# Early weight parts at listed places, stored from ScalarE's queue; layer 1's modulation pieces further apart; two squares summed on TensorE

## The chip, the cores and the metric

One NeuronCore of a Trainium2 chip runs the kernel. The metric is the device time of one execution in microseconds (us); the time of a kernel is the median of its runs. The profile is of one further execution, with a time of its own. A core's engines work side by side: TensorE (PE; its weight loads are listed as PEld) for matrix products, VectorE (DVE), ScalarE (ACT) and GpSimd (POOL) for elementwise work, SyncE (SP), whose queue issues most transfers.

## The reference

Two layers over two streams of 256 tokens by 1024 features in float32: the latent stream `x` and a context stream `ctx`. Each layer is a modulated RMSNorm, a mixer with a gated residual, and a modulated RMSNorm with a gated ConvFFN. Layer 0's mixer is a bidirectional retention with four heads, layer 1's a bidirectional recurrent block (RG-LRU).

```python
silu_c, silu_cc = jax.nn.silu(c), jax.nn.silu(c_ctx)
for i in range(DEPTH):
    need_ctx = i < DEPTH - 1
    mod_l = (silu_c @ ada_w[i] + ada_b[i])[:, None, :]
    mod_c = silu_cc @ ada_w[i] + ada_b[i]
    sh1, sc1, g1, sh2, sc2, g2 = jnp.split(mod_l, N_MOD, axis=-1)
    ...
    h_l = modulate(rmsnorm(x, norm_mix[i]), sh1, sc1)
    h_c = modulate(rmsnorm(ctx, norm_mix[i]), csh1, csc1)
    out_c, out_l = ...
    x = x + g1 * out_l
    ...
    x = x + g2 * conv_ffn(modulate(rmsnorm(x, norm_ffn[i]), sh2, sc2), ...)
    ...
return rmsnorm(x, final_norm)
```

## The kernel before

The features lie on the 128 partitions and the tokens of both streams side by side, 512 columns in all (`NT`), 256 of each stream (`NS`). Each weight matrix is cut into blocks of 128 by 128. A float32 product is made of three faster ones: the weight is split into a high part (`whi`) and a low part (`wlo`), the activation likewise, and `mm3` (L515 to L518) multiplies high by high, high by low and low by high into one sum (`ps`).

The weights are streamed in the order in which they are used, in units of eight blocks (1024 columns, 512 KB). SyncE's queue loads a unit into one of nine `raw` buffers (L394); ScalarE casts it to `whi` (L417), VectorE subtracts to get `wlo` (L449), and TensorE multiplies it into the activations. A raw buffer can be loaded again when its last reader is done, and the loads stand in one order on SyncE's queue. `make_plan` (L88) writes this order down: the list `PIECES`, with marks every 16 blocks. Beside the blocks it puts two other kinds of pieces there.

- **Modulation pieces** ("ada"). The rows of `ada_w` are multiplied by the two condition vectors: ScalarE scales 512 columns (L570, L573), GpSimd adds the result to a sum (L574). Up to four such products are taken from the queue `adaq` at each tick; a tick comes once per matrix product of eight blocks (`tick`, L356). At the end the sums go through TensorE with a ones vector (`total`, L588), are copied by ScalarE (`down`, L601) and transposed by four small products (`up`, L607) into `mod`. `need` waits, in the program's order, until a group is done. `L1` sets where the two groups of layer 1 (l1 for the mixer, f1 for the FFN) are read: l1 from block 576 on, every 16 blocks, f1 from 768 on.
- **Early weight parts** ("pre"). The recurrent block's own 40 units (130 to 169) are loaded and split long before they are used, when there is time, written back to memory and later loaded as ready parts (`kept`, L482). ScalarE casts the high part (L467), VectorE subtracts the low part (L474) and copies back some blocks of 32 rows (L477), and SyncE stores both at once (L482). `pre_piece` (L453) queues these as three steps of `preq`, one per tick, and the store two ticks later (`keepq`). `PRE = (64, 48)` reads a piece (two units) at blocks 64, 112, 160 and so on to 976.

A gemm of layer 0's FFN is followed on VectorE by the two side taps of a convolution (`cv`, L1182 and L1183), a product of gate and value (L1191) and the low part of that (`fzlo`, L539).

At the end of the retention and of layer 0's FFN the next RMSNorm's sum of squares is built: ScalarE squares each of eight chunks (`sq`, L653), GpSimd adds them up (L659) but for the last one, and TensorE sums over the partitions with a matrix of ones (`st`, L663 for the sum, L665 for the last square). ScalarE takes the root (`sd`, L671), VectorE the reciprocal (`rstd`, L673). `direct` is the number of squares that TensorE takes without GpSimd. `staged_out` (L1027) does the last part of such a matrix for one stream after the other (s = 0, then 1), `staged_in` the first part of the next.

Of the kernel before, what the change touches and what calls it, by code (L numbers as in the profile page):

```python
# [12 lines left out]
P = 128  # L13
# [47 lines left out]
L1 = (64,16,256,16)  # L61
# [34 lines left out]
def make_plan():  # L96
# [78 lines left out]
    for n, i in enumerate(range(first, last, 16)):  # L175
        early.setdefault((PRE[0] + PRE[1] * n) // 16 * 16, []).append(i)
# [84 lines left out]
PRE = (64, 48)  # L261
# [34 lines left out]
class Net:  # L296
# [59 lines left out]
    def tick(self, n=1):  # L356
# [8 lines left out]
        if self.keepq and self.keepq[0][0] <= self.now:  # L365
            self.keepq.popleft()[1]()
# [11 lines left out]
    def load(self, upto):  # L378

        while self.nload <= min(upto, len(LOADS) - 1):  # L380
# [10 lines left out]
            while any(t <= n - RAWS for t, _ in self.preq):  # L391
                self.preq.popleft()[1]()
            r = self.wp.tile([P, UNIT], F32, tag="raw", name=f"raw{pi}{'ab'[h]}", bufs=RAWS)
# [59 lines left out]
    def pre_piece(self, pi):  # L453

        nc = self.nc
        rs = [self.half(pi, h) for h in range(2)]
        st = {}

        def hi(h, u):
            while len(self.keepq) > 1:  # L460
                self.keepq.popleft()[1]()
            st[h] = t = self.wp.tile([P, 2, UNIT], F32R, tag="pre", name=f"pre{u}", bufs=2)
            r, o = rs[h], 0
            cuts = [(a, n) for kind, a, n in self.runs(u) if kind == "main"] + [(UNIT, UNIT)]
            for a, n in cuts:
                if a > o:
                    nc.scalar.copy(t[:, 0, o:a], r[:, o:a])  # L467
                if n > a:
                    nc.scalar.copy(t[:, 0, a:n].bitcast(F32), r[:, a:n])
                o = n  # L470

        def lo(h, u):
            t = st[h]
            nc.vector.tensor_tensor(t[:, 1, :], rs[h], t[:, 0, :].bitcast(F32), ALU.subtract)  # L474
            for kind, a, n in self.runs(u):
                if kind == "left":
                    nc.vector.tensor_copy(t[64:96, 0, a:n], t[64:96, 1, a:n])  # L477
            self.keepq.append((self.now + 2, lambda: keep(h, u)))

        def keep(h, u):  # L480
            self.kept[u] = self.dp.tile([P, 2, UNIT], F32, tag=f"kept{u}", name=f"kept{u}")
            nc.sync.dma_start(self.kept[u], st[h].bitcast(F32))  # L482

        u = PIECES[pi][1] // 8
        a, b = (PLACE[pi, h][1] for h in range(2))
# [160 lines left out]
    def stats_begin(self, direct=1):  # L646
# [380 lines left out]
    def staged_out(self, name, ks, ms, rhs, layer, p, nxt):  # L1027
# [6 lines left out]
        for s in range(2):  # L1034
            sl = slice(s * NS, (s + 1) * NS)
            for i, m in enumerate(ms):
# [12 lines left out]
                self.residual(ps[:, :NS], layer, p, m, s)  # L1049
                self.stats_add(m, s)  # L1050
# [732 lines left out]
```

## Time and profile before

| | |
|---|---|
| time, median of 3 runs | 1240.64 us (1240.56 to 1242.41) |
| the profiled execution: time, span | 1242.04 us, 1240.2 us |
| TensorE: busy, mean granted clock | 1190.2 us (96%), 0.984 |
| VectorE, ScalarE, GpSimd: busy | 899.3 us (73%), 730.9 us (59%), 365.5 us (29%) |
| chain that ended last: TensorE, VectorE, DMA | 74%, 15%, 4% |

An engine's busy time is the sum over its instructions, and a share of it is an average over stages with different limits. The chain that ended last is followed back from the last instruction: each piece of it is what the next one waited for. Where TensorE's own instructions are the chain, nothing held it. The time of a run is some 2 us above the span, for what lies before the first and after the last instruction.

### The profile page before, as it was taken

What the parts mean: (1) busy time and instruction counts of PE and PEld (TensorE: products, weight loads), DVE (VectorE), ACT (ScalarE), POOL (GpSimd) and SP (SyncE); (2) the same over time, 40 slices, a digit from 0 to 9 for tenths busy, and PEclk for the clock granted to TensorE, in tenths of its full rate; (3) what the DMA queues carried; (4) which work ended last, traced back from release to release, by engine and by line L of the source; (5) the groups of instructions that cost most, each with busy time, mean ns of one, the idle gap of its engine ahead of it and who ended that gap; (6) DMA issues with size and microseconds to landing.
All of it is one profiled execution on the core that took longest, in us unless ns stands there. A gap on an engine that the chain in (4) does not pass through costs nothing.

```text
span 1240.2 us, 17983 instructions
## 1 busy us (share of the span) xinstructions
PE 1190.2 (96%) x6760; PEld 1012.2 (82%) x6760; DVE 899.3 (73%) x1285; ACT 730.9 (59%) x1098; POOL 365.5 (29%) x242
## 2 busy tenths in 40 slices
PE   8999799999979998988999999999999999999997
PEld 4678688778868888876778887879989888999996
DVE  5665977895596578899953678743758877988843
ACT  5456466765654444878754676432397856766542
POOL 0000545558160022489954355221000001000010
PEclk9999899999999999999989999999999999999999
DMA  9963577377355254577688688744576895555531
GB/s 327 337 236 133 172 265 242 119 270 256 101 171 204 97 210 141 200 270 256 220 314 286 232 286 291 252 136 136 185 288 220 310 324 186 172 187 185 190 117 34
DMA packets 73399, 265.37 MB, mean 214 GB/s; under 512 B 8672, under 2 KB 12384, under 8 KB 68192
## 3 DMA queue, kind: packets, MB, share of 16 engines
q1 hardware_dynamic: 72736, 263.70, 61.9%
q8 instruction: 53, 0.87, 0.3%
q10 hardware_dynamic: 576, 0.52, 0.1%
q14 instruction: 34, 0.28, 0.1%
HBM read 219.62 MB, written 42.99 MB: 212 GB/s over the span
## 4 chain that ended last, share of the span: by engine, by line
PE 74%; DVE 15%; DMA 4%; issue 3%; ACT 3%; SPq 1%; POOL 0%; DVEq 0%; ACTq 0%; POOLq 0%
PE ps L516 21%; PE ps L517 20%; PE ps L518 20%; DVE wlo L449 4%; PE ps L940 2%; PE ps L941 2%; PE ps L942 2%; DVE pre L474 1%; DVE zlo L539 1%; PE av L517 1%; PE av L516 1%; PE av L518 1%; DVE fzlo L539 1%; DVE cv L1182 1%; DVE zt L1001 1%
## 5 line engine op out<-in xcount | busy, mean ns | idle before, releaser
L574 POOL TENSOR_TENSOR ada<-ada,adap 128x512 f32<-128x512 f32 x196 | 323.3, 1674 | 351.3 <-ACT adap L573 212.4
L518 PE MATMUL ps<-hhi,wlo 128*128 128x512 f32 (+1 forms) x640 | 245.8, 384 | 13.3 <-DVE wlo L449 13.3
L516 PE MATMUL ps<-hhi,whi 128*128 128x512 f32 (+1 forms) x640 | 249.2, 389 | 0.0
L517 PE MATMUL ps<-hlo,whi 128*128 128x512 f32 (+1 forms) x640 | 244.7, 382 | 0.0
L659 POOL TENSOR_TENSOR sq<-sq,sq 128x256 f32<-128x256 f32 x33 | 38.7, 1181 | 500.9 <-ACT sq L653 500.4
L517 PE MATMUL ps<-hx,whi 128*128 128x256 f32 x592 | 168.1, 284 | 0.4 <-DVE hx L692 0.2
L516 PE MATMUL ps<-hx,whi 128*128 128x256 f32 x592 | 168.2, 284 | 0.2 <-ACT hx L691 0.2
L518 PE MATMUL ps<-hx,wlo 128*128 128x256 f32 x592 | 167.5, 283 | 0.0
L518 PEld LDWEIGHTS ps<-hhi,wlo 128*128 128x128 f32 x640 | 122.0, 191 | 39.9 <-DVE wlo L449 16.9
L516 PEld LDWEIGHTS ps<-hhi,whi 128*128 128x128 f32 x640 | 122.3, 191 | 31.4 <-issue 4.9
L517 PEld LDWEIGHTS ps<-hlo,whi 128*128 128x128 f32 x640 | 122.1, 191 | 23.0 <-issue 1.0
L516 PEld LDWEIGHTS ps<-hx,whi 128*128 128x128 f32 x592 | 113.5, 192 | 4.2 <-issue 2.5
L517 PEld LDWEIGHTS ps<-hx,whi 128*128 128x128 f32 x592 | 113.5, 192 | 1.2 <-DVE hx L692 0.8
L518 PEld LDWEIGHTS ps<-hx,wlo 128*128 128x128 f32 x592 | 113.5, 192 | 0.0
L1179 ACT ACTIVATE cv<-ps,par 128x512 f32<-128x512 f32 (+1 forms) x88 | 58.7, 668 | 59.7 <-PE ps L518 59.7
L1182 DVE SCALAR_TENSOR_TENSOR cv<-ps,par,cv 128x510 f32<-128x510 f32 (+1 forms) x88 | 53.9, 612 | 47.8 <-ACT cv L1179 47.5
L516 PE MATMUL ps<-fzhi,whi 128*128 128x512 f32 (+1 forms) x198 | 74.0, 374 | 4.1 <-ACT fzhi L538 4.1
L517 PE MATMUL ps<-fzlo,whi 128*128 128x512 f32 (+1 forms) x198 | 73.3, 370 | 0.0
L518 PE MATMUL ps<-fzhi,wlo 128*128 128x512 f32 (+1 forms) x198 | 73.1, 369 | 0.0
L702 DVE SCALAR_TENSOR_TENSOR xc<-ps,mod,xc 128x256 f32<-128x256 f32 x48 | 23.0, 479 | 60.9 <-PE ps L518 60.9
L518 PE MATMUL ps<-zhi,wlo 128*128 128x512 f32 (+1 forms) x152 | 55.9, 368 | 6.7 <-DVE wlo L449 6.7
L517 PE MATMUL ps<-zlo,whi 128*128 128x512 f32 (+1 forms) x152 | 55.7, 366 | 2.6 <-DVE zlo L539 2.6
(777 smaller groups left out, 2794.0 us busy)
## 6 DMA issues: line engine op xcount, KB each, us to landing
kept<-pre SPq DMA_DIRECT2D x40, 1024.0 KB, 5.2
whi<-kept SPq DMA_DIRECT2D x40, 512.0 KB, 4.7
wlo<-kept SPq DMA_DIRECT2D x40, 512.0 KB, 5.8
ak<-wpk SPq DMA_DIRECT2D x32, 256.0 KB, 6.6
xc<-xt SPq DMA_DIRECT2D x4, 256.0 KB, 3.4
x<-xt SPq DMA_DIRECT2D x4, 256.0 KB, 5.6
xst<-xhi SPq DMA_DIRECT2D x16, 64.0 KB, 4.2
cst<-cst SPq DMA_DIRECT2D x3, 192.0 KB, 4.9
```

What stands on the lines that cost most here:

```text
L449: self.eng(e).tensor_tensor(d[q, o:n], r[q, o:n], hi[q, o:n].bitcast(F32), ALU.subtract)
L516: mm(ps, w[0], x[0], start=start, stop=False)
L517: mm(ps, w[0], x[1], start=False, stop=False)
L518: mm(ps, w[1], x[0], start=False, stop=stop)
L539: self.lag(lambda: self.nc.vector.tensor_tensor(lo, src, hi.bitcast(F32), ALU.subtract))
L574: nc.gpsimd.tensor_tensor(acc[i, s], acc[i, s], t, ALU.add)
L659: nc.gpsimd.tensor_tensor(self.acc[s], self.acc[s], sq, ALU.add)
L940: mm(pss[t], xh, wh, start=k == 0, stop=False)
L941: mm(pss[t], xh, wl, start=False, stop=False)
L942: mm(pss[t], xl, wh, start=False, stop=k == KD - 1)
L1179: nc.scalar.activation(acc, ps[:, :n], AF.Identity, scale=w(1), bias=self.pc("fcb", layer * 44 + f))
L1182: nc.vector.scalar_tensor_tensor(a3[:, :, 1:], p3[:, :, :NS - 1], w(0), a3[:, :, 1:], ALU.mult, ALU.add)
```

## The change

Five edits:

1. `L1` puts layer 1's modulation pieces 20 blocks apart (rounded down to 16): l1 at blocks 528 to 752 and f1 at 768 to 992.
2. `PRE` becomes a list of twenty blocks: 80, 96, 112, then four from 176, four from 304, four from 416, then 720, 752, 784, 944, 976.
3. An early unit's low part is written over its raw buffer; the high parts have tiles of half the size, four in place of two. The store is two transfers of 512 KB on ScalarE's queue, a tick after the subtraction in place of two. A store is issued earlier if a load needs the raw buffer.
4. `direct` is 2 by default, so that the last two squares of a sum go to TensorE (at two places; the others name their number).
5. In `staged_out` ScalarE takes the root of a constant [128, 1] just before the last square of the first stream.

```diff
-L1 = (64,16,256,16)
+L1 = (24, 20, 264, 20)
...
-        early.setdefault((PRE[0] + PRE[1] * n) // 16 * 16, []).append(i)
+        early.setdefault(PRE[n], []).append(i)
...
-PRE = (64, 48)
+
+PRE = (80, 96, 112, 176, 192, 208, 224, 304, 320, 336, 352, 416, 432, 448, 464, 720, 752, 784, 944, 976)
...
-        if self.keepq and self.keepq[0][0] <= self.now:
-            self.keepq.popleft()[1]()
+        while self.keepq and self.keepq[0][1] <= self.now:
+            self.keepq.popleft()[2]()
...
+            while self.keepq and self.keepq[0][0] <= n - RAWS:
+                self.keepq.popleft()[2]()
...
+        places = [PLACE[pi, h][1] for h in range(2)]
...
-            while len(self.keepq) > 1:
-                self.keepq.popleft()[1]()
-            st[h] = t = self.wp.tile([P, 2, UNIT], F32R, tag="pre", name=f"pre{u}", bufs=2)
+            while len(self.keepq) > 3:
+                self.keepq.popleft()[2]()
+            st[h] = t = self.wp.tile([P, UNIT], F32R, tag="pre", name=f"pre{u}", bufs=4)
...
-            t = st[h]
-            nc.vector.tensor_tensor(t[:, 1, :], rs[h], t[:, 0, :].bitcast(F32), ALU.subtract)
+
+            t, r = st[h], rs[h]
+            nc.vector.tensor_tensor(r.bitcast(F32R), r, t.bitcast(F32), ALU.subtract)
...
-                    nc.vector.tensor_copy(t[64:96, 0, a:n], t[64:96, 1, a:n])
-            self.keepq.append((self.now + 2, lambda: keep(h, u)))
+                    nc.vector.tensor_copy(t[64:96, a:n], r[64:96, a:n])
+            self.keepq.append((places[h], self.now + 1, lambda: keep(h, u)))
...
-            self.kept[u] = self.dp.tile([P, 2, UNIT], F32, tag=f"kept{u}", name=f"kept{u}")
-            nc.sync.dma_start(self.kept[u], st[h].bitcast(F32))
+            self.kept[u] = k = self.dp.tile([P, 2, UNIT], F32, tag=f"kept{u}", name=f"kept{u}")
+            nc.scalar.dma_start(k[:, 0, :], st[h].bitcast(F32))
+            nc.scalar.dma_start(k[:, 1, :], rs[h])
...
-    def stats_begin(self, direct=1):
+    def stats_begin(self, direct=2):
...
+                if (s, m) == (0, ms[-1]):
+                    self.nc.scalar.activation(self.const([P, 1], name="sqrt"), self.eps, AF.Sqrt)
                 self.stats_add(m, s)
```

The edits move instructions on every engine; three places show it. Lines of the changed kernel are 3 to 8 higher than before (the low part of the weights L452 for L449, an early low part L479 for L474, its copies L482 for L477). In the rows a name is followed by its unit or buffer number.

The first place is VectorE between the reciprocal of the third head's statistics (`rstd`) and the first two products of its readout (`zt`), before:

```order
L673 RECIPROCAL rstd_474_3031<-sd_473_3029 128x512
L449 TENSOR_TENSOR wlo45_3044<-raw51b_2872,whi45_2975 128x1024
L474 TENSOR_TENSOR pre143_3006<-raw50b_2800,pre143_3006 128x1024
L449 TENSOR_TENSOR wlo46_3086<-raw53a_3034,whi46_3042 128x1024
L1001 SCALAR_TENSOR_TENSOR zt_486_3126<-av_457_2909,par_10_89,rstd_474_3031 128x512
L1002 TENSOR_TENSOR zt_486_3126<-zt_486_3126,sg_414_2608 128x512
L1001 SCALAR_TENSOR_TENSOR zt_489_3132<-av_459_2924,par_10_89,rstd_474_3031 128x512
L1002 TENSOR_TENSOR zt_489_3132<-zt_489_3132,sg_456_2907 128x512
```

and changed:

```order
L679 RECIPROCAL rstd_474_3107<-sd_473_3105 128x512
L452 TENSOR_TENSOR wlo45_3120<-raw55b_2946,whi45_3051 128x1024
L479 TENSOR_TENSOR raw54a_2827<-raw54a_2827,pre150_3082 128x1024
L482 CAST pre150_3082<-raw54a_2827 32x256
L452 TENSOR_TENSOR wlo46_3168<-raw57a_3110,whi46_3118 128x1024
L479 TENSOR_TENSOR raw54b_2871<-raw54b_2871,pre151_3156 128x1024
L482 CAST pre151_3156<-raw54b_2871 32x256
L1007 SCALAR_TENSOR_TENSOR zt_486_3208<-av_457_2985,par_10_89,rstd_474_3107 128x512
L1008 TENSOR_TENSOR zt_486_3208<-zt_486_3208,sg_414_2657 128x512
L1007 SCALAR_TENSOR_TENSOR zt_489_3214<-av_459_3000,par_10_89,rstd_474_3107 128x512
L1008 TENSOR_TENSOR zt_489_3214<-zt_489_3214,sg_456_2983 128x512
```

Unit 143's early low part has gone from there, and those of units 150 and 151 have come, each with a copy.

The second place is VectorE in layer 0's up product, from the low part of unit 74 on, some 530 us into the program, before:

```order
L449 TENSOR_TENSOR wlo74_4789<-raw75a_4723,whi74_4729 128x1024
L539 TENSOR_TENSOR fzlo_690_4776<-cv_666_4592,fzhi_689_4775 128x512
L474 TENSOR_TENSOR pre152_4772<-raw74a_4719,pre152_4772 128x1024
L477 COPY pre152_4772<-pre152_4772 32x256
L1182 SCALAR_TENSOR_TENSOR cv_699_4835<-ps_692_4784,par_10_89,cv_699_4835 128x2x255
L1183 SCALAR_TENSOR_TENSOR cv_699_4835<-ps_692_4784,par_10_89,cv_699_4835 128x2x255
L449 TENSOR_TENSOR wlo75_4850<-raw75b_4725,whi75_4787 128x1024
L539 TENSOR_TENSOR fzlo_698_4833<-cv_667_4596,fzhi_697_4832 128x512
L474 TENSOR_TENSOR pre153_4830<-raw74b_4721,pre153_4830 128x1024
L1182 SCALAR_TENSOR_TENSOR cv_707_4890<-ps_700_4839,par_10_89,cv_707_4890 128x2x255
L1183 SCALAR_TENSOR_TENSOR cv_707_4890<-ps_700_4839,par_10_89,cv_707_4890 128x2x255
L1191 TENSOR_TENSOR cv_699_4835<-cv_699_4835,cv_707_4890 128x512
```

and changed:

```order
L452 TENSOR_TENSOR wlo74_4932<-raw80a_4871,whi74_4877 128x1024
L545 TENSOR_TENSOR fzlo_707_4919<-cv_680_4743,fzhi_706_4918 128x512
L1190 SCALAR_TENSOR_TENSOR cv_716_4974<-ps_709_4927,par_10_89,cv_716_4974 128x2x255
L1191 SCALAR_TENSOR_TENSOR cv_716_4974<-ps_709_4927,par_10_89,cv_716_4974 128x2x255
L452 TENSOR_TENSOR wlo75_4989<-raw80b_4873,whi75_4930 128x1024
L545 TENSOR_TENSOR fzlo_715_4972<-cv_681_4747,fzhi_714_4971 128x512
L1190 SCALAR_TENSOR_TENSOR cv_723_5025<-ps_717_4978,par_10_89,cv_723_5025 128x2x255
L1191 SCALAR_TENSOR_TENSOR cv_723_5025<-ps_717_4978,par_10_89,cv_723_5025 128x2x255
L1199 TENSOR_TENSOR cv_716_4974<-cv_716_4974,cv_723_5025 128x512
```

The two early low parts and the copy are gone; the rest keeps its order. In the changed kernel no early part stands from unit 66 to unit 90.

The third place is ScalarE at the end of the retention's output, over the last squares of the latent stream and the context stream's first root, before:

```order
L653 ACTIVATE sq_604_4085<-xc_4_77 128x256
L653 ACTIVATE sq_606_4104<-xc_5_79 128x256
L653 ACTIVATE sq_608_4121<-xc_5_79 128x256
L671 ACT_TABLE_LOAD
L671 ACTIVATE sd_611_4130<-st_610_4127,eps_49_178 128x256
```

and changed:

```order
L659 ACTIVATE sq_604_4200<-xc_4_77 128x256
L659 ACTIVATE sq_606_4219<-xc_5_79 128x256
L1057 ACT_TABLE_LOAD
L1057 ACTIVATE sqrt_608_4235<-eps_49_178 128x1
L659 ACTIVATE sq_609_4237<-xc_5_79 128x256
L677 ACTIVATE sd_612_4247<-st_611_4243,eps_49_178 128x256
```

The table load for the root stands before the last square instead of behind it.

## Rows read from the trace of the kernel before

**Rows 1.** The page, busy time of an engine, share of the span, instructions
```profile
PE 1190.2 (96%) x6760; PEld 1012.2 (82%) x6760; DVE 899.3 (73%) x1285; ACT 730.9 (59%) x1098; POOL 365.5 (29%) x242
```

**Rows 2.** TensorE's waits: us in all, times, the longest
```profile
PE ps L518 <- DVE wlo L449: 20.0, 9, 6.0
PE st L663 <- POOL sq L659: 5.7, 3, 4.1
PE ps L516 <- ACT fzhi L538: 4.1, 1, 4.1
PE ps L517 <- DVE zlo L539: 2.6, 1, 2.6
...
PE adat L638 <- ACT krow L631: 1.5, 2, 1.0
```

**Rows 3.** Stretches: length, each engine's busy us (instructions), granted clock, DMA share, GB/s
```profile
340.00:380.00 40.00, 33.46 (x143) 26.53 (x142) 39.35 (x52) 22.95 (x40) 21.92 (x13) 0.96 0.52 172
420.00:440.00 20.00, 20.00 (x93) 16.66 (x92) 19.58 (x37) 9.10 (x12) 0.00 (x0) 1.00 0.61 219
460.00:500.00 40.00, 35.32 (x273) 34.58 (x273) 28.62 (x50) 20.66 (x36) 8.47 (x7) 0.96 0.41 132
520.00:640.00 120.00, 108.51 (x454) 86.47 (x453) 108.65 (x88) 88.41 (x131) 103.44 (x61) 0.94 0.76 263
640.00:840.00 200.00, 200.00 (x890) 162.00 (x889) 128.59 (x146) 109.46 (x152) 85.17 (x53) 1.00 0.72 248
```

**Rows 4.** VectorE in time, 530 to 545 us: start, us, instruction
```profile
530.59 2.32 DVE L449 TENSOR_TENSOR wlo<-raw75a,whi 128x1024 fp32r<-128x1024 f32 x1
...
536.89 1.26 DVE L477 CAST pre<-pre 32x256 fp32r<-32x256 f32 x1
```

**Rows 5.** VectorE in time, 425 to 427 us
```profile
425.48 1.22 DVE L474 TENSOR_TENSOR pre<-raw60b,pre 128x1024 fp32r<-128x1024 f32 x1
426.73 0.28 DVE L477 CAST pre<-pre 32x256 fp32r<-32x256 f32 x1
```

**Rows 6.** The stretch 520 to 640 us, line 474 alone
```profile
520.00:640.00 120.00, 12.78 (x6) 0.94 0.76 263
```

**Rows 7.** The stretch 520 to 640 us, line 477 alone
```profile
520.00:640.00 120.00, 5.24 (x5) 0.94 0.76 263
```

**Rows 8.** The chain that ended last, 500 to 640 us: start, us, what
```profile
543.54 7.65 DMA raw80b<-wpk
...
615.43 2.23 DVE pre L474
617.69 1.45 DVE pre L477 x2
...
622.18 0.80 PE ps L516
```

**Rows 9.** All engines in time, 474 to 481.5 us
```profile
475.46 4.18 POOL L659 TENSOR_TENSOR sq<-sq,sq 128x256 f32<-128x256 f32 x1 [0.38 <-ACT sq L653]
...
479.69 0.70 PE L663 MATMUL st<-sq,ones_d 128*128 128x256 f32 x2 [4.06 <-POOL sq L659]
...
480.23 1.02 PE L665 MATMUL st<-sq,ones_d 128*128 128x256 f32 x2
```

**Rows 10.** ScalarE in time, around 462 us and around 858 us
```profile
461.15 0.42 ACT L653 ACTIVATE sq<-xc 128x256 f32<-128x256 f32 x1 [0.50 <-DVE xc L702]
461.58 1.28 ACT L671 ACT_TABLE_LOAD   x1
462.88 0.47 ACT L671 ACTIVATE sd<-st,eps 128x256 f32<-128x256 f32 x1
...
857.72 0.42 ACT L653 ACTIVATE sq<-xc 128x256 f32<-128x256 f32 x1 [3.54 <-DVE xc L702]
```

**Rows 11.** The instructions on tile adarow: count, ns least/median/most, starts
```profile
L601 ACT COPY adarow<-ada x4: 576/582/587, 122.9 to 826.9; 128x512 f32<-128x512 f32 x4
```

**Rows 12.** The page, DMA issues: count, KB each, us to landing
```profile
kept<-pre SPq DMA_DIRECT2D x40, 1024.0 KB, 5.2
```

More of the change, by code (lines that the diff above doesn't have):

```diff
@@ L466, in hi @@
                 if a > o:
-                    nc.scalar.copy(t[:, 0, o:a], r[:, o:a])
+                    nc.scalar.copy(t[:, o:a], r[:, o:a])
                 if n > a:
-                    nc.scalar.copy(t[:, 0, a:n].bitcast(F32), r[:, a:n])
+                    nc.scalar.copy(t[:, a:n].bitcast(F32), r[:, a:n])
                 o = n
         def lo(h, u):
-            t = st[h]
-            nc.vector.tensor_tensor(t[:, 1, :], rs[h], t[:, 0, :].bitcast(F32), ALU.subtract)
+            t, r = st[h], rs[h]
+            nc.vector.tensor_tensor(r.bitcast(F32R), r, t.bitcast(F32), ALU.subtract)
             for kind, a, n in self.runs(u):
                 if kind == "left":
-                    nc.vector.tensor_copy(t[64:96, 0, a:n], t[64:96, 1, a:n])
-            self.keepq.append((self.now + 2, lambda: keep(h, u)))
+                    nc.vector.tensor_copy(t[64:96, a:n], r[64:96, a:n])
+            self.keepq.append((places[h], self.now + 1, lambda: keep(h, u)))
         def keep(h, u):
-            self.kept[u] = self.dp.tile([P, 2, UNIT], F32, tag=f"kept{u}", name=f"kept{u}")
-            nc.sync.dma_start(self.kept[u], st[h].bitcast(F32))
+            self.kept[u] = k = self.dp.tile([P, 2, UNIT], F32, tag=f"kept{u}", name=f"kept{u}")
+            nc.scalar.dma_start(k[:, 0, :], st[h].bitcast(F32))
+            nc.scalar.dma_start(k[:, 1, :], rs[h])
         u = PIECES[pi][1] // 8
-        a, b = (PLACE[pi, h][1] for h in range(2))
+        a, b = places
         self.preq.extend([(a, lambda: hi(0, u)), (b, lambda: (lo(0, u), hi(1, u + 1))), (b, lambda: lo(1, u + 1))])
```

## The prediction

> **What bounds the kernel now.** I read the page's busy times first. TensorE is busy for 1190.2 of 1240.2 us [rows 1], so only what stops it or slows its clock can be won. The reader should then ask where it stops, and the list of what TensorE waited for answers that: VectorE's low parts of the weights hold it for 20.0 us in nine places, one square that GpSimd adds for 4.1, a ScalarE cast for 4.1 and a low part of the readout for 2.6 [rows 2]. Third comes the table by stretches, which puts a place to them. I count a stretch's loss as the time that TensorE was not busy, and the share of the clock that was not granted times the stretch (its two levels are 1.2 and 2.4 GHz).
>
> - 520 to 640 us: 11.5 idle and 0.06 x 120 = 7.2 of clock, 18.7 in all [rows 3]. VectorE is busy for 108.65 and GpSimd for 103.44 of 120.
> - 340 to 380 us: 6.5 + 1.6 = 8.1. 460 to 500 us: 4.7 + 1.6 = 6.3 [rows 3].
> - 420 to 440 us: no loss, with VectorE at 19.58 of 20, so this place has no room left. 640 to 840 us: no loss, VectorE at 64% [rows 3].
>
> Last, VectorE's own instructions in these places. A subtraction of 1024 columns takes 2.32 us while GpSimd adds modulation products, and 1.22 where GpSimd is idle; the small 32-row copy takes 1.26 against 0.28 [rows 4, 5]. In the two stretches in question an early weight part therefore costs two to four times what it costs in a quiet one.
>
> **Part 1, the stage from 520 to 640 us.** Before, six early halves with five rows of copies sit there: 12.78 + 5.24 = 18.0 us of VectorE [rows 6, 7]. After, none is left (the second order place). What stays is 108.65 - 18.0 = 90.6 us, against the 120 - 18.7 = 101.3 us that TensorE needs at full pace: 89%, between the 91% at which it loses 18.7 and the 64% at which it loses nothing. The chain of waits shows the link: a subtraction of 2.23 and two copies of 1.45 stand right before the cast for which TensorE stops at 622 us [rows 8]. A load that ended last for 7.65 us at 543 us was also on the chain [rows 8]; its buffer came free when a modulation product was done, and these now come every 20 blocks instead of 16, so that the eight additions of a piece, about 1.7 us each (103.44 us for 61 [rows 3]), meet 20 blocks' worth of products (13 us, at 5.2 for eight blocks) rather than 16 (10.4). I take three quarters of the ceiling: **-14**. Ends: -18.7 (all of it), and -7 (only the stop at 622 us goes: the 3.7 us of parts ahead of it, and half of the clock's 7.2).
>
> **Part 2, two squares to TensorE.** At 475.46 us GpSimd's last addition took 4.18 us while VectorE subtracted without pause, and TensorE stood still for 4.06 [rows 9]; the clock loss behind it is the 1.6 above. With the last two squares fed straight to TensorE the last GpSimd addition is one that started earlier and ran in under a microsecond. Gain 4.06 + 1.6 = 5.7. Against it: one more ones-product in each of the two statistics; from one to the next it took 480.23 - 479.69 = 0.54 [rows 9], 1.1 for two. And the dummy square root brings its table load ahead of the last square of the first half: that square started at 461.15 after ScalarE had been idle for 0.50 [rows 10]; the load of 1.28 can start with that idle time, at 460.65, so the square starts at about 462.0, and TensorE's statistics, which wait for it in order, come 0.85 later. Net **-3.8**; ends -5.7 and -2.
>
> What a table switch costs is read from the rows: the load starts at 461.58, as the square ends, takes 1.28, and the root starts at 462.88 [rows 10], so nothing else is lost around it. The Trainium skill (ScalarE: Activation LUTs, "What ACT_TABLE_LOAD costs") gives about 2.66 us for each switch, the load of 1283 ns and a drain of 1380 ns. By that the square would come 1.4 us later still and this part would be -2.4; no drain shows in these rows.
>
> The same edit at the end of layer 0's FFN costs two more products, **+1.1**; the table load falls into 3.54 us in which ScalarE is idle [rows 10] and is free.
>
> **Part 3, the third head's readout (335 to 380 us).** Between the reciprocal and the readout's first products VectorE had one early half; it now has two, with a copy each (the first order place). GpSimd still adds here (21.9 of 40 us) and VectorE is never idle (39.35 of 40) [rows 3], so each is charged at the contended price: 2.32 + 2 x 1.26 = **+4.8**. Ends: +1.8 (quiet prices, 1.22 + 2 x 0.28 [rows 5]) and +7 (another stretch of half clock, as the 1.6 in this window).
>
> **Part 4, the fourth head's readout (412 to 450 us).** Four halves with copies now stand among the readout's products where before there were two and one further on. GpSimd is idle, so they cost the quiet 1.22 and 0.28 [rows 5], about 4 us in a stretch that is 98% busy but where TensorE did not wait [rows 3]. Most of this is covered by how far the low parts run ahead of their products (some 5 us); if that cover is gone, they come late one by one. **+1**; ends 0 and +5. Heads 1 and 2 exchange one half for another at about the same place: 0.
>
> **Part 5, the last modulation pieces.** With their new marks the last two pieces are read just before the recurrent block, so the sum of layer 1's FFN modulation, its copy and the four transposed products now fall after the block's first products, with nothing of TensorE's queue between. The nearest row is the same chain at the program's start: TensorE waited up to 1.0 us for such a copy [rows 2]; the copy here is twice as wide (0.58 [rows 11]). **+1.2**; ends +0.5 and +3.
>
> **Part 6, the stores.** SP's waits for a subtraction before it stores go to ScalarE's queue, as 80 issues one tick later. Behind them stand the casts of the next high parts, but the subtraction was put in line a tick earlier (24 products, 24 x 20 / 93 = 5.2 us [rows 3]) and is mostly over, so they don't wait: 0 on the path. The raw buffer, though, is now held until the store has landed, and fifteen of the twenty pieces stand in four dense groups (marks 80 to 112, 176 to 224, 304 to 352, 416 to 464). I put **+0.5** on loads that come late for it; ends 0 and +5. The five pieces from block 720 on lie where TensorE lost nothing and VectorE has a third free: 0.
>
> **The sum.** -14 - 3.8 + 1.1 + 4.8 + 1 + 1.2 + 0.5 = -9.2. Against the profiled execution's 1242.04 that is 1232.8. The runs' median, 1240.64, lies 1.4 lower, and so does my time: **1231.4 us**. A measurement of this kernel tells 0.2% (2.5 us) from no change.
>
> **The rivals.**
> - *Contention stays, and the stage keeps its stops.* Part 1 gives only its lower end, -7. For it: GpSimd has as many modulation additions as before, at 1.7 us each they fill nearly all of 13 us per piece, so VectorE's remaining 2.32 us subtractions stay slow. The Trainium skill (GPSIMD Engine Reference, "Key points") says that GpSimd shares its SBUF interfaces with VectorE and that instructions with two SBUF inputs contend, by which moving the pieces elsewhere leaves the rest as slow. The 2.32 against 1.22 agrees with that [rows 4, 5]. Against it: 18 us of VectorE's work leave. Time: 1231.4 + 7 = 1238.4. Chance 0.15, about half of it beyond 0.2%.
> - *The raw ring becomes the bound* (slower). A half used to give its buffer back when the subtraction ended; now it waits a tick (5.2) and a store's landing (5.2 for the whole megabyte [rows 12]), some 10 us more. Nine buffers at four to six loads in 16 blocks (10.4 us) come round in 16 to 23 us, and a half that waits for its cast, its subtraction and its store can hold one for as long. Then each dense piece delays a later block's load, its cast and its low part, and TensorE stops for it. From 9.2 / 15 = 0.6 us per dense piece on, nothing is gained; at 1.6 us each it is 1231.4 + 24 - 0.5 = 1255, at 1.0 us 1246. For it: loads stood on the chain already [rows 8]. Against: where two of the dense groups fall DMA moves 172 and 219 GB/s, and 263 in the busiest stretch [rows 3], so the transfers themselves have room. Chance 0.12; its middle is 1248.
> - *The dummy root's switch costs 2.66 us*, as in the skill's rule above: with 1.4 more on the path, 1232.8. Chance 0.05.
>
> **How the numbers follow.** My forecast has 0.68, its own range being 1225 to 1237. The first rival reaches to 1239, and the unknown ends of parts 3, 4 and 6 upward to 1241; below, part 1's ceiling and part 3's quiet price give 1231.4 - 4.7 - 3.0 = 1223.7. So 1223 to 1241. Faster: 0.68 + 0.05 + half of 0.15, less 0.02 for ends that meet: 0.78. Slower: the ring, 0.11 of it beyond the bound. The same: 0.11.
>
> **What would show it.** Right: between 520 and 640 us no early subtraction, VectorE below 91% and TensorE's idle time under 4 us; no wait for GpSimd's square at the first statistics; a longer stop in the third head's readout, for VectorE, near 350 us; a wait of about a microsecond for the copied modulation row at the recurrent block's start. Wrong: waits of SP for a store on ScalarE's queue followed by late casts in the dense groups (the ring); subtractions still at 2.3 us and waits for low parts of over 8 us between 520 and 640 (contention).

## The result and the profile after

The changed kernel takes **1223.56 us** (median of 4 runs, 1223.15 to 1226.73) against 1240.74 us before in the same comparison: a ratio of 0.9864, with a 95% interval from 0.9845 to 0.9883. That is 17.2 us faster. The forecast was 1231.4 with a range of 1223 to 1241, so the sign was right and the gain was nearly twice the 9.2 us of the sum; the time lies 0.6 us inside the lower end of that range, and below the 1225 to 1237 that the prediction called the forecast's own. The profiled execution took 1223.15 us, its span is 1221.4 us, 18.8 shorter than before, and the mean granted clock 0.988.

The first view is the table by stretches of the changed kernel, with the columns of [rows 3]. The stretches are the same times as before. Up to 460 us the program is near the same point in them (between 0.8 us behind and 2.4 ahead); it is 3.5 us further at 480 us and 21 at the end of layer 0's FFN.

```profile
120.00:160.00 40.00, 33.75 (x137) 26.56 (x136) 37.40 (x52) 21.51 (x36) 18.05 (x12) 0.87 0.49 173
240.00:260.00 20.00, 18.43 (x80) 14.56 (x80) 19.67 (x36) 9.52 (x19) 6.32 (x5) 1.00 0.51 172
340.00:380.00 40.00, 32.96 (x132) 26.50 (x131) 39.18 (x55) 22.43 (x38) 19.36 (x12) 0.87 0.58 197
420.00:440.00 20.00, 20.00 (x94) 16.67 (x93) 19.16 (x36) 11.92 (x15) 0.00 (x0) 1.00 0.78 283
460.00:500.00 40.00, 39.88 (x305) 38.36 (x304) 30.39 (x51) 25.18 (x45) 8.60 (x10) 1.00 0.27 87
500.00:520.00 20.00, 18.01 (x80) 14.59 (x78) 13.20 (x14) 20.00 (x31) 20.00 (x14) 1.00 0.57 181
520.00:640.00 120.00, 118.33 (x524) 95.48 (x525) 100.15 (x88) 81.14 (x117) 90.95 (x54) 1.00 0.64 216
```

By the prediction's measure (idle time and the clock's share) the stretch from 520 to 640 us fell from a loss of 18.7 to 1.7 us, and 2.0 us appeared just ahead of it, between 500 and 520, where TensorE had lost nothing before. 460 to 500 us fell from 6.3 to 0.1. The third head (340 to 380 us) rose from 8.1 to 7.0 + 0.13 x 40 = 12.2; this is an upper figure, because idle time at half clock is counted twice in it, as in every figure of this measure that has a share of the clock. 420 to 440 us, which had no room left on VectorE, still loses nothing.

What TensorE waited for, in the changed kernel (columns as in [rows 2]):

```profile
PE ps L524 <- DVE wlo L452: 18.5, 9, 6.0
...
PE st L669 <- POOL sq L665: 1.0, 1, 1.0
...
PE adat L613 <- ACT adarow L607: 0.7, 1, 0.7
```

The low parts hold TensorE for almost as long as before (18.5 against 20.0 us), but less of it lies between 500 and 640 us (3.7 against 7.4). The stops for the cast and for the readout's low part [rows 2] are gone, and one stop of 1.0 us for the squares is left of 5.7. The predicted wait for the copied modulation row is there, at 0.7 us.

### The profile page after: what moved, and what is told of

The parts are those of the page before. It is cut to its first block, busy times and chain, and to the rows that moved or that the text cites. A ratio compares the mean times of both kernels' runs of the same rounds, so it can differ in the third digit from the quotient of the medians.

```text
span 1221.4 us, 18028 instructions
## 1 busy us (share of the span) xinstructions
PE 1186.3 (97%) x6768; PEld 1010.2 (83%) x6768; DVE 892.5 (73%) x1285; ACT 731.9 (60%) x1100; POOL 360.0 (29%) x238
## 4 chain that ended last, share of the span: by engine, by line
PE 78%; DVE 12%; ACT 3%; DMA 3%; issue 2%; SPq 1%; DVEq 0%; ACTq 0%
PE ps L522 22%; PE ps L524 22%; PE ps L523 22%; DVE wlo L452 3%; PE ps L946 2%; PE ps L947 2%; PE ps L948 2%; DVE rstd L679 1%; ACT adap L579 1%; DVE fzlo L545 1%; PE av L524 1%; PE av L523 1%; PE av L522 1%; DVE zt L1007 1%; PE ps L1639 1%
## 5 line engine op out<-in xcount | busy, mean ns | idle before, releaser
L665 POOL TENSOR_TENSOR sq<-sq,sq 128x256 f32<-128x256 f32 x29 | 32.4, 1127 | 472.9 <-ACT sq L659 382.9
L1190 DVE SCALAR_TENSOR_TENSOR cv<-ps,par,cv 128x510 f32<-128x510 f32 (+1 forms) x88 | 53.9, 613 | 61.7 <-ACT cv L1187 61.7
L1191 DVE SCALAR_TENSOR_TENSOR cv<-ps,par,cv 128x510 f32<-128x510 f32 (+1 forms) x88 | 54.2, 616 | 3.1
```

Of the source, the lines that this page charges most:

```text
L665: nc.gpsimd.tensor_tensor(self.acc[s], self.acc[s], sq, ALU.add)
L1190: nc.vector.scalar_tensor_tensor(a3[:, :, 1:], p3[:, :, :NS - 1], w(0), a3[:, :, 1:], ALU.mult, ALU.add)
L1191: nc.vector.scalar_tensor_tensor(a3[:, :, :NS - 1], p3[:, :, 1:], w(2), a3[:, :, :NS - 1], ALU.mult, ALU.add)
```

## The experiments

Twelve kernels were run. All times are medians; a ratio is against the kernel before, in the same comparison. Unless it is said otherwise, an edit starts from the changed kernel.

### Taking the parts of the change back one by one

**Layer 1's modulation pieces at their old places.**

```diff
-L1 = (24, 20, 264, 20)
+L1 = (64, 16, 256, 16)
```

> The changed kernel (1223.6 us) with layer 1's modulation pieces back at every 16 blocks. Theory A (between 520 and 640 us the early weight parts on VectorE were the bound, and their leaving made the gain): 0 to 4 us are lost, about 1225.5. Rival B (the modulation pieces' pace was the bound there, through GpSimd's backlog and the raw buffers that it holds): 8 us or more are lost, 1231.5 or more, with loads and low parts late between 520 and 640 us again.

Measured: 1217.65 us, ratio 0.9818 (0.9799 to 0.9837). Both theories missed: it is 5.9 us *faster* than the changed kernel. The two stretches in this kernel:

```profile
500.00:520.00 20.00, 20.00 (x90) 16.57 (x89) 17.79 (x18) 19.43 (x30) 15.21 (x10) 1.00 0.49 158
520.00:640.00 120.00, 120.00 (x537) 97.51 (x535) 104.13 (x85) 85.66 (x124) 111.91 (x64) 1.00 0.69 229
```

TensorE loses nothing, although GpSimd is busier than in either of the other two (111.91 of 120 us; 103.44 before, 90.95 changed). So the new marks of `L1`, whose spacing the prediction had counted as a help, cost time, and GpSimd's additions alone are no bound. Where the cost arises, the changed kernel's chain that ended last shows, 500 to 522 us (some of the longer pieces: start, us, what):

```profile
501.86 2.47 ACT adap L579 x4
504.32 1.33 ACT cv L1187 x2
508.94 1.34 ACT ada L576 x2
516.57 1.49 DVE cv L1199
```

and VectorE's and TensorE's waits there:

```profile
512.73 0.75 DVE L1190 SCALAR_TENSOR_TENSOR cv<-ps,par,cv 128x510 f32<-128x510 f32 x1 [3.12 <-ACT cv L1187]
...
520.32 0.50 PE L524 MATMUL ps<-hhi,wlo 128*128 128x512 f32 x1 [2.31 <-DVE wlo L452]
```

Up to 512.7 us the chain is ScalarE's, from there on VectorE's. The modulation products (`adap`) of the pieces that are now read from block 528 on stand ahead of the convolution's first step (`cv`), for which VectorE was idle for 3.12 us, and TensorE stops behind that at 520 us. In the kernel with the old `L1` the same chain is TensorE's own products alone. ScalarE's busy share does not tell the two apart: it is 20.00 of 20 us here and 19.43 there.

**Only the FFN's pieces (f1) back.**

```diff
-L1 = (24, 20, 264, 20)
+L1 = (24, 20, 256, 16)
```

> The changed kernel with the FFN's modulation pieces (f1) back at every 16 blocks, the mixer's (l1) left at every 20 from block 528. Theory J (the loss against the old places comes from l1's early start, where its products fill ScalarE's queue between 500 and 520 us and hold up the casts): 1 to 1.5 us faster than the changed kernel (the copied row's wait at the recurrent block's start goes), about 1222.3. Rival K (it is f1's late end that costs): 1218.

Measured: 1223.44 us, ratio 0.9850 (0.9833 to 0.9866). f1's late end is not what costs (rival K wanted 1218); the 1.3 us expected from the copied row's wait were not to be seen in the median either: in its profile the recurrent block's part is 1.7 us shorter than in the changed kernel, and layer 0's FFN 2.1 us longer. By the medians nearly all of the 5.9 us belongs to l1's marks; whether to their earlier start or to their wider spacing, no run separates. The stops at 520 and 555 us are in its profile as in the changed kernel's; all that TensorE waits between 500 and 640 us makes 3.7 us of it. Where the rest lies stays open.

**The early parts at their old marks.**

```diff
-PRE = (80, 96, 112, 176, 192, 208, 224, 304, 320, 336, 352, 416, 432, 448, 464, 720, 752, 784, 944, 976)
+PRE = (64, 112, 160, 208, 256, 304, 352, 400, 448, 496, 544, 592, 640, 688, 736, 784, 832, 880, 928, 976)
```

> The changed kernel with the early weight parts at the old marks (every 48 blocks from 64), all else as changed. Theory A: the stage from 520 to 640 us loses 12 us or more again, the second head some 2.5 us, and the third head some 3 us less than in the changed kernel: in all 11 to 14 us lost, about 1236. Rival B: at most 4 us lost, under 1228.

Measured: 1247.28 us, ratio 1.0053 (1.0034 to 1.0072). It is 23.7 us slower than the changed kernel and slower than the kernel before. Theory A had the right place and too small a size:

```profile
460.00:500.00 40.00, 34.72 (x252) 32.62 (x251) 29.16 (x48) 22.79 (x42) 11.23 (x11) 0.96 0.48 160
520.00:640.00 120.00, 107.70 (x450) 85.24 (x449) 105.56 (x93) 85.18 (x124) 82.62 (x49) 0.93 0.74 255
```

The stage loses 12.3 + 8.4 = 20.7 us again, and the stretch before it 6.9. All the other edits of the change, without the new list, cost 6.6 us (against 1240.65 in that comparison). Over half of it comes at the end of the retention, where the two reciprocals (`rstd`) stand 22.1 us apart, and 18.5 before. GpSimd's stop for the squares is gone there; the chain that ended last shows what came in its place:

```profile
479.43 1.11 ACT ada L576 x2
...
480.57 3.78 ACT adap L579 x6
...
485.29 0.38 ACT sd L677
```

ScalarE scales modulation products, which the new `L1` has read earlier, ahead of the second root.

**The new list alone, in the kernel before.**

```diff
-        early.setdefault((PRE[0] + PRE[1] * n) // 16 * 16, []).append(i)
+        early.setdefault(PRE[n], []).append(i)
...
-PRE = (64, 48)
+PRE = (80, 96, 112, 176, 192, 208, 224, 304, 320, 336, 352, 416, 432, 448, 464, 720, 752, 784, 944, 976)
```

> The kernel before (1240.7 us) with the new list of marks for the early parts alone; low parts in tiles of their own (two), one store on SyncE two ticks later. Theory A (the places make the gain, the way of storing only serves it): 9 to 14 us faster than before, about 1229. Rival G (with two tiles and a store that is two ticks late, the dense groups stall ScalarE and the loads): at most 4 us faster, 1237 or more.

Measured: 1218.44 us, ratio 0.9816 (0.9800 to 0.9832): 23.4 us faster than the kernel before, and faster than the changed kernel. Two tiles and one late store on SyncE serve the dense groups well enough, so rival G falls. The list is worth 23.4 us in the kernel before and 23.7 in the changed one; it is the whole gain. Its two stretches, and the early subtractions alone in the second:

```profile
460.00:500.00 40.00, 37.59 (x294) 36.52 (x293) 31.33 (x53) 22.89 (x38) 7.11 (x8) 1.00 0.28 95
520.00:640.00 120.00, 120.00 (x536) 97.52 (x535) 105.83 (x86) 90.02 (x130) 111.56 (x65) 1.00 0.69 229
```

```profile
520.00:640.00 120.00, 8.16 (x4) 1.00 0.69 229
```

So the stretch is not free of early parts. Since the program is further on, the pieces from block 720 fall into its end, from 609 us on (from 605 with the old `L1`, from 609 in the changed kernel, which has three of 4.76 us in all). Before, the six took 12.78 us [rows 6], and four of them lay between 534 and 581 us. What the list changes is less how much of this work the stretch holds than where it stands.

**The squares and the dummy root.**

```diff
-    def stats_begin(self, direct=2):
+    def stats_begin(self, direct=1):
...
-                if (s, m) == (0, ms[-1]):
-                    self.nc.scalar.activation(self.const([P, 1], name="sqrt"), self.eps, AF.Sqrt)
```

> The changed kernel with one square instead of two straight to TensorE and without the dummy square root. Theory A (the last GpSimd addition, slowed by VectorE, holds TensorE at the end of the retention): the stop of about 4 us and its stretch of half clock come back, 4 to 6 us lost, about 1228.5. Rival C (that stop came only from an early part beside the addition, which has gone from there): 0, within 1 us of the changed kernel.

Measured: 1225.64 us, ratio 0.9883 (0.9862 to 0.9903): 2.1 us slower than the changed kernel, between the two theories, and the two intervals overlap. In the stretch TensorE is idle for 2.4 us there and for 0.1 in the changed kernel:

```profile
460.00:500.00 40.00, 37.60 (x297) 36.65 (x296) 29.78 (x50) 23.12 (x40) 10.36 (x10) 1.00 0.30 93
```

What TensorE waited for between 455 and 482 us in this kernel:

```profile
PE st L669 <- POOL sq L665: 2.4, 2, 1.7
```

The stop for GpSimd's last addition comes back at 1.7 us, not at 4.1 [rows 2], and TensorE keeps its full clock. In the kernel before, an early half stood beside that addition; the list had already taken it away. So the first part of rival C holds: with the list alone the longest stop is 1.7 us as well. With the squares alone (the old marks, above) it is gone altogether, so either edit takes most of it away. In these profiles the reciprocals at the retention's end stand 15.8 us apart, against 14.7 in the changed kernel, and those at the end of layer 0's FFN 13.1 against 14.0, so that the squares and the root gain 1.1 us in the one place and cost 0.9 in the other. That they are worth 2.1 us of the whole time is not shown.

**The dummy root alone.**

```diff
-                if (s, m) == (0, ms[-1]):
-                    self.nc.scalar.activation(self.const([P, 1], name="sqrt"), self.eps, AF.Sqrt)
```

> The changed kernel without the dummy square root. The prediction's term (the table load, put ahead of the last square, makes TensorE wait 0.85 us longer at the first statistics): 0.5 to 1.2 us faster, about 1222.7. Rival E (the load was on the path of the root behind it, and its earlier place saves that): 0.5 to 1.5 us slower, about 1224.6.

Measured: 1224.11 us, ratio 0.9862 (0.9840 to 0.9883), not to be told from the changed kernel; neither expectation is decided by the time, and the reciprocals there stand 14.7 us apart in both. ScalarE's rows show why. First the changed kernel, then this one:

```profile
460.18 0.42 ACT L659 ACTIVATE sq<-xc 128x256 f32<-128x256 f32 x1 [1.11 <-DVE xc L708]
460.62 1.28 ACT L1057 ACT_TABLE_LOAD   x1
461.91 0.20 ACT L1057 ACTIVATE sqrt<-eps 128x1 f32<-128x1 f32 x1
462.02 0.40 ACT L659 ACTIVATE sq<-xc 128x256 f32<-128x256 f32 x1
463.21 0.47 ACT L677 ACTIVATE sd<-st,eps 128x256 f32<-128x256 f32 x1 [0.79 <-PE st L671]
```

```profile
459.16 0.42 ACT L659 ACTIVATE sq<-xc 128x256 f32<-128x256 f32 x1 [1.11 <-DVE xc L708]
460.51 0.42 ACT L659 ACTIVATE sq<-xc 128x256 f32<-128x256 f32 x1 [0.94 <-DVE xc L708]
460.95 1.28 ACT L677 ACT_TABLE_LOAD   x1
462.24 0.47 ACT L677 ACTIVATE sd<-st,eps 128x256 f32<-128x256 f32 x1
```

From the square that ends first in each to the root `sd` it is 463.21 - 460.18 = 3.03 us with the dummy and 462.24 - 459.16 = 3.08 without: the load is only moved from behind the last square to ahead of it.

**The stores on SyncE's queue.**

```diff
-            nc.scalar.dma_start(k[:, 0, :], st[h].bitcast(F32))
-            nc.scalar.dma_start(k[:, 1, :], rs[h])
+            nc.sync.dma_start(k[:, 0, :], st[h].bitcast(F32))
+            nc.sync.dma_start(k[:, 1, :], rs[h])
```

> The changed kernel with the two stores of an early unit on SyncE's queue instead of ScalarE's. Theory A (the queue does not matter, since the loads behind a store wait for buffers anyway): within 1.5 us of the changed kernel. Rival D (a store that waits on SyncE for its subtraction holds up the loads behind it in the dense groups): 4 us or more lost, 1227.5 or more.

Measured: 1224.64 us, ratio 0.9877 (0.9852 to 0.9902), 1.1 us from the changed kernel and inside its interval. Theory A's time holds; its reason was not tried. SyncE does wait before its stores again, and it costs nothing that can be measured:

```profile
SPq L487 <- DVE pre L482: 75.0, 12, 21.1
```

### Is it the early parts, or GpSimd beside them?

**The kernel before without GpSimd's additions for the mixer's modulation.** The early parts stay where they were. This kernel leaves these additions out: each sum keeps only its first product.

```diff
-                nc.gpsimd.tensor_tensor(acc[i, s], acc[i, s], t, ALU.add)
+                if name != "l1":
+                    nc.gpsimd.tensor_tensor(acc[i, s], acc[i, s], t, ALU.add)
```

> The kernel before without GpSimd's additions for layer 1's mixer modulation: each sum keeps only its first product (ScalarE still makes the others). Theory A in its full form (the early parts are a bound between 520 and 640 us only because GpSimd's additions double VectorE's times): subtractions there take 1.2 us, TensorE's loss there falls from 18.7 to under 5 us although the early parts stay; about 1226. Rival H (the number of instructions on VectorE is the bound, with or without GpSimd): over 10 us of the loss stay, 1233 or more.

One execution: 1221.35 us. Theory A's full form holds, with a time some 5 us under its own, and rival H falls. The stretch, and then VectorE in time in the same kernel:

```profile
520.00:640.00 120.00, 120.00 (x537) 97.51 (x536) 75.29 (x96) 95.27 (x140) 0.00 (x0) 1.00 0.85 306
```

```profile
559.22 1.22 DVE L449 TENSOR_TENSOR wlo<-raw82a,whi 128x1024 fp32r<-128x1024 f32 x1
560.35 1.22 DVE L474 TENSOR_TENSOR pre<-raw81a,pre 128x1024 fp32r<-128x1024 f32 x1
562.57 0.75 DVE L1183 SCALAR_TENSOR_TENSOR cv<-ps,par,cv 128x510 f32<-128x510 f32 x1 [1.00 <-ACT cv L1180]
...
565.16 0.68 DVE L539 TENSOR_TENSOR fzlo<-cv,fzhi 128x512 fp32r<-128x512 f32 x1
```

The 18.7 us are gone with the early parts in place, just as they go when the early parts leave the stage's first 85 us and GpSimd stays. Neither is the bound; the two together are. That the additions hold up loads through their buffers, as rival B of the first experiment has it, is no cause of its own: with the list alone GpSimd is busier than before (111.56 us) and nothing is lost.

VectorE's busy share of the stretch does not tell the kernels apart, because a stopped TensorE also brings it less work: with the list alone it is 105.83 of 120 us for 536 products and nothing is lost, with the old marks 105.56 for 450, and 20.7 us are. Set against the time that TensorE needs at full pace (120 us less the loss), as the prediction did for the changed kernel, it does. This estimate from the rows above and [rows 3] gives 107% before, 106% with the old marks, 85% changed, 87% with the old `L1`, 88% with the list alone and 63% here.

### The third head

**The piece at block 352 moved to 736.**

```diff
-PRE = (80, 96, 112, 176, 192, 208, 224, 304, 320, 336, 352, 416, 432, 448, 464, 720, 752, 784, 944, 976)
+PRE = (80, 96, 112, 176, 192, 208, 224, 304, 320, 336, 416, 432, 448, 464, 720, 736, 752, 784, 944, 976)
```

> The changed kernel with the piece at block 352 (units 150 and 151, in the third head's readout) moved to 736, the later ones in their order. Theory A (those halves and copies stand in VectorE's chain ahead of the readout's products and add about 3 us to TensorE's stops there): 2.5 to 5 us faster, 1218.5 to 1221. Rival F (the stops there come from the readout itself and the modulation additions, or the other pieces take the place): within 1 us of the changed kernel.

Measured: 1221.43 us, ratio 0.9841 (0.9821 to 0.9861), 2.1 us less than the changed kernel: under theory A's 2.5 and over rival F's 1, with intervals that overlap. The waits show that both have a part in it. Between 340 and 380 us the changed kernel waits first, then this one:

```profile
PE ps L524 <- DVE wlo L452: 7.0, 2, 4.0
```

```profile
PE ps L524 <- DVE wlo L452: 5.3, 1, 5.3
```

The first stop goes, the second grows from 4.0 to 5.3 us. VectorE's rows in the changed kernel show why the two halves cost less than predicted:

```profile
337.80 2.31 DVE L479 TENSOR_TENSOR raw54a<-raw54a,pre 128x1024 fp32r<-128x1024 f32 x1
340.14 0.28 DVE L482 CAST pre<-raw54a 32x256 fp32r<-32x256 f32 x1
...
341.60 1.22 DVE L479 TENSOR_TENSOR raw54b<-raw54b,pre 128x1024 fp32r<-128x1024 f32 x1
342.85 0.29 DVE L482 CAST pre<-raw54b 32x256 fp32r<-32x256 f32 x1
```

Only the first half ran beside an addition; the second and both copies had the quiet prices.

**Both: the old `L1` and the moved piece.** The edits of the first and the last experiment together.

> The changed kernel with layer 1's modulation back at its old places (which alone gave 1217.7) and the piece at block 352 moved to 736 (which alone gave 1221.4). Theory A (two separate places, 500 to 560 us and 340 to 380 us): the gains add, about 1215.5. Rival I (the second only moves the stop to the next wait of the same head): no better than 1217.7.

Measured: 1216.15 us, ratio 0.9795 (0.9781 to 0.9810). It is the fastest of the complete kernels here, 7.4 us under the changed one. Against the old `L1` alone (1217.65) it is 1.5 us less, less than the intervals tell apart, so that the two gains add is not shown.

**The same without GpSimd's additions for layer 0's FFN modulation.** This kernel leaves these additions out: each sum keeps only its first product.

```diff
-                nc.gpsimd.tensor_tensor(acc[i, s], acc[i, s], t, ALU.add)
+                if name != "f0":
+                    nc.gpsimd.tensor_tensor(acc[i, s], acc[i, s], t, ALU.add)
```

> The first kernel of this call without GpSimd's additions for layer 0's FFN modulation (each sum keeps only its first product). Theory L (the stops of the third head at 350 to 365 us come from VectorE beside GpSimd's additions): the loss of about 8 us between 340 and 380 us falls under 3, about 1209. Rival M (the readout's own chain on VectorE is too long there): 6 us or more of it stay, 1213 or more.

One execution: 1197.86 us, 11 less than theory L said. It starts from the kernel with both edits, the "first kernel" of the text above. The first and the third head in it:

```profile
120.00:160.00 40.00, 37.28 (x165) 29.99 (x164) 36.60 (x65) 28.16 (x45) 0.00 (x0) 1.00 0.66 222
340.00:380.00 40.00, 40.00 (x187) 32.40 (x186) 28.98 (x52) 20.76 (x33) 0.00 (x0) 1.00 0.60 200
```

The third head's loss is gone, and rival M with it. The rest of the 18 us comes from places that the expectation had left out: the first head loses 2.7 us, where the kernel with both edits has 7.0 of idle time and 0.09 x 40 = 3.6 of clock. In both heads it is VectorE beside these additions that holds TensorE, and the readout's chain alone is short enough in the third.

**The FFN's pieces of layer 0 every 16 blocks.** A way to keep these additions and have them done before the third head; again from the kernel with both edits.

```diff
-    ada("f0", 128, 24)
+    ada("f0", 128, 16)
```

> The first kernel of this call with layer 0's FFN modulation pieces every 16 blocks instead of 24, so that they end at block 304, before the third head's readout. Theory L: the third head's stops shrink by 5 us or more, and the second head, which now has them beside its early parts, loses 0 to 3: 1211 to 1214. Rival N (the denser products cost as much in the first two heads as they free in the third): within 1.5 us of the first kernel.

Measured: 1222.23 us, ratio 0.9846 (0.9830 to 0.9863), 6.1 us more than without it. The third head loses nothing, as theory L has it, but the second loses more than that, beyond what rival N allowed:

```profile
200.00:280.00 80.00, 67.30 (x289) 51.42 (x289) 65.50 (x79) 55.19 (x87) 51.47 (x33) 0.96 0.67 238
340.00:380.00 40.00, 40.00 (x182) 32.93 (x181) 31.84 (x64) 20.10 (x32) 0.00 (x0) 1.00 0.43 143
```

Between 200 and 280 us 12.7 us are idle and 3.2 go to the clock; in the kernel with both edits 1.7 are idle and none go to the clock. GpSimd is now busy there for 51 of 80 us (43 without the edit), beside four early halves of the group from block 176 on.

## Why the prediction was right, and where its sum was off

The direction came from the right reading: the stage from 520 to 640 us was the largest loss, VectorE, slowed by GpSimd's additions, was its bound, and the early parts left its dense part. That the time fell into the range owes something to luck, since two errors hid each other: the list gives 23 us, more than the sum has for everything, and the new `L1`, counted as a help, takes 5.9 of them back.

The loss by stretches counts some time twice. A mark that every kernel passes in the same order counts nothing twice: the start of VectorE's reciprocal of a norm's statistics. Time from each to the next in us, from one profile of each kernel:

| from, to | before | changed | list alone | changed, old `L1` |
|---|---|---|---|---|
| start, first head | 123.1 | 122.4 | 123.0 | 121.8 |
| first, second head | 104.3 | 105.8 | 105.6 | 105.2 |
| second, third head | 107.7 | 104.5 | 104.4 | 104.6 |
| third, fourth head | 85.1 | 87.9 | 87.7 | 86.6 |
| fourth head, retention's end | 43.2 | 43.2 | 43.2 | 43.2 |
| the two at the retention's end | 18.5 | 14.7 | 15.9 | 14.7 |
| to layer 0's FFN's end | 378.0 | 360.3 | 358.7 | 357.8 |
| the two there | 13.0 | 14.0 | 13.0 | 13.9 |
| to the recurrent block's end | 163.0 | 164.0 | 160.8 | 161.0 |

From there to the last reciprocal it is 196.4 us in all four.

Point by point:

- **Part 1 (-14).** Layer 0's FFN gained 17.7 us, of which 1.6 are the half clock that the prediction put to part 2: 16.1. The size is near, the make-up is not. The list alone gains 19.4 there (17.8 without the 1.6), nearly the ceiling of 18.7 and not three quarters. The prediction placed its 89% between the 91% that lost 18.7 us and the 64% that lost nothing, but the 91% is of the time that passed and the 89% of the time at full pace; by the latter measure the kernel before had 107%, so 89% lay well on the safe side. And the step "these now come every 20 blocks instead of 16, so that the eight additions of a piece, about 1.7 us each (103.44 us for 61 [rows 3]), meet 20 blocks' worth of products" counted the new `L1` as a help by GpSimd's pace; it costs 5.9 us of the whole time. Of the 3.7 that the traces place, the stop of 2.31 us at 520 us has ScalarE in its chain, where pieces that are read earlier put their products ahead of the convolution's first steps. The first sign of being right, no early subtraction between 520 and 640 us, did not hold to the letter: three stand at the end of that stretch.
- **Part 2 (-3.8).** With the half clock behind it, the place gained 3.9 + 1.6 = 5.5 us. Most of it, 2.7 + 1.6, came with the list alone, which the prediction had not credited for it; the squares and the root add 1.1 to 1.2. The 0.85 us put down for the table load did not come: it moved as worked out, from behind the last square to ahead of it, and the marks are 14.7 us apart with the dummy root and without. At the FFN's end the two more products cost 1.0 us (**+1.1** in the sum).
- **Part 3 (+4.8).** The third head took 2.8 us more. The stops are there, as predicted, but "GpSimd still adds here (21.9 of 40 us) and VectorE is never idle (39.35 of 40) [rows 3], so each is charged at the contended price" was too dear: three of the four instructions had the quiet price, and from the reciprocal to the readout's first product it took 0.9 us more than before (10.5 against 9.6), not 4.8. Moving the piece away gains 2.1 us of the time.
- **Part 4 (+1), part 6 (+0.5).** No loss at 420 to 440 us, with VectorE at 19.16 of 20; no load of the dense groups shows as a loss. Part 5 (+1.2) shows as a wait of 0.7 us, and between the marks there it is 1.0; moving f1 back changes the median by 0.1.
- **Heads 1 and 2 (0).** The second gained 3.2 us, the first lost 1.5. Some of the latter is the profile's own: with the old `L1`, which changes nothing there, the clock in that stretch is 0.91 and not 0.87.

So nearly every term came out better than it was put down, each by some 2 us at most, and the second head, put at nothing, gave 3.2; no single one makes the difference between 9.2 and 17.2. Profiles of kernels that are alike in a head differ there by up to 1.3 us, so the small terms are no surer than that.

The raw ring as the bound is refuted: the changed kernel with the old `L1`, which holds the raw buffers until the stores have landed, takes 1217.65 us, and the list alone, which gives them back at the subtraction, 1218.44. The rival of contention was wrong as a forecast (the stage did lose its stops) and right as a mechanism: with the list alone GpSimd was busier than before, in the changed kernel at 90.95 of 120 us, and the subtractions beside it stayed at 2.1 to 2.3 us. VectorE has the time for them once the early parts are out of the way.

What the in-place low part and the smaller tiles do for themselves was not tried alone. The list in the kernel before (1218.44) and the changed kernel with the old `L1` (1217.65) differ by the stores, tiles, squares and root together, and by less than their intervals.

## What to carry to other kernels

A busy share of the time that passed does not say whether an engine is the bound: VectorE at 88% cost nothing in one kernel here and 20.7 of 120 us in another. Set its work against the time that the critical engine needs at full pace: over 100% lost time here, 85 to 88% little or none. When work can be done at any time, put it where the engine has room, and count its price beside the engines that run there, since the same subtraction cost 1.2 us in one stage and 2.3 in another. Take a change of several edits apart before keeping it: here one of five edits made the whole gain, one took a quarter of it back, and what the others gave is too small to be told one by one. Reading data earlier is not free even when its consumer is off the critical path: here each piece brought a burst of products to ScalarE's queue, ahead of steps that others waited for.

## What the runs showed of the hardware

Beside GpSimd's additions VectorE's subtractions of two tiles took 1.7 to 2.6 times as long, and the convolution's taps, which read a matrix product's sum, did not. In the kernel with the old `L1`, where GpSimd is busy without a break (start, us, instruction):

```profile
557.79 2.13 DVE L452 TENSOR_TENSOR wlo<-raw84b,whi 128x1024 fp32r<-128x1024 f32 x1
559.85 1.78 DVE L545 TENSOR_TENSOR fzlo<-cv,fzhi 128x512 fp32r<-128x512 f32 x1
561.55 0.74 DVE L1190 SCALAR_TENSOR_TENSOR cv<-ps,par,cv 128x510 f32<-128x510 f32 x1
```

In the kernel without those additions the same three took 1.22, 0.68 and 0.75 us (rows above). The rule of the Trainium skill (GPSIMD Engine Reference, "Key points"), that VectorE and GpSimd contend where a VectorE instruction is in a 2-port perf mode or has two inputs in SBUF, the memory of the tiles, fits these rows: the tap has one of its two in PSUM, where a product's sum lies. A copy of 32 rows went from 0.28 to 1.26 us [rows 4, 5], the largest ratio here; it has one input, and no run shows in which mode it ran.

A switch of ScalarE's table cost its load of 1.28 us and 0.01 to the next instruction (461.91 - 460.62 = 1.29), not the 2.66 us that the Trainium skill gives (ScalarE: Activation LUTs, "What ACT_TABLE_LOAD costs"); here the measurement decides.
